# An encoder block's last two weight blocks of a chunk, multiplied two row tiles at a time

## The chip, the cores and the metric

The program runs on one core of one Trainium2 chip. The metric is the device time in microseconds (us) of one execution of the whole program. The engines are named as in the profile: PE (TensorE, matrix products), PEld (its weight loads), DVE (VectorE), ACT (ScalarE), POOL (GpSimd) and SP (SyncE, which here only issues DMAs). PE writes into PSUM, of which the kernel uses eight banks of 128 x 512 floats; all else lies in SBUF.

## The reference

One layer of a hybrid encoder on 512 tokens of width 2048, all in float32, cut to what matters:

```python
h = rmsnorm(x, g_mix)
qa, ka, va, qb, kb, vb = split(h @ w_in)             # w_in: 2048 x 4608
out_a = rmsnorm(mixer_a(qa, ka, va), g_out_a)        # 8 heads of 128, 2 kv heads, axial rotary
out_b = rmsnorm(mixer_b(qb, kb, vb), g_out_b)        # 8 heads, three dilated windows, partial rotary
x = x + concat(out_a, out_b) @ w_out                 # 2048 x 2048
gate, up = split(rmsnorm(x, g_ffn) @ w_gate_up)      # 2048 x 2 * 5632
x = x + (silu(gate) * up) @ w_down
return rmsnorm(x, g_final)
```

## The kernel before, in words

**Products.** Each float32 operand is split into a high and a low part of a faster type; ACT writes the high part (a copy that rounds), DVE the low part (the difference). A product is then three matmuls (`mm3`, L235 to L237). The 512 tokens are four row tiles of 128 (`NT = 4`). The work on PE is a list of *units*: one weight block of 128 rows by 512 columns against the four row tiles, twelve matmuls.

**Chunks.** A chunk is a run of units that add into the same four PSUM banks, one bank for each row tile. Units 0 to 63 are the four chunks qkB0 to qkB3 (`in_plain`, `in_chunk`), 16 units each: the queries and keys of two B heads per chunk. Units 64 to 95 are the four A chunks of W_out (`out_chunk` with kind "A"), 8 units each, A0 to A3. (The trace's chunks that are made of column blocks, before and behind these, are numbered apart.) Behind them come four B chunks of W_out, then the gate, up and down projections.

**Attention beside the chunks.** The attention of the 16 heads is cut into *head slots*, four a head. The loop at the end of the program runs a unit, then as many side tasks as a credit allows (1.42 a unit up to qkB3's end, 1.9 from A0 on, against a cost of 1.5 for a slot of an A head and 1.2 for one of a B head), so that one slot stands between most units, sometimes two, sometimes none. A slot issues, in this order: `pt` (four transposes of softmax rows, L582, into a bank; ACT copies it as `pTh`, L226, DVE makes `pTl`, L227), `pv` (three matmuls that add into the head's output bank), at a head's end `fin` (ACT: `oT` L599, its store L602, `sq` L608 or, for a mixer's first head, `acc` L605), `score` (three matmuls; for an A head DVE's maximum L567 and ACT's exponential L568, for a B head DVE's masked row L571 and ACT's exponential L573; then DVE's L575 and L576), and at times `tq` or `tk` (transposes of the next head's query and key, L544 and L555). The softmax rows of a slot are transposed six slots later, the transposed rows are multiplied two slots after that.

**What orders the work.** Each engine runs its instructions in the order of the program. `bank()` takes the oldest free bank from a queue of eight and `release` puts it at the end; a chunk holds four, a head's output one, and three are left for `pt`, `score`, `tq` and `tk`. A bank's next writer waits until its last reader is done. Small SBUF tiles (`slot`: p, pTh, pTl, qTh, oT, sq, acc, evqkB, x and so on) share one space; a tile takes the place of an older one, and its first writer waits until the older one's last reader is done, a DMA store among them.

**A chunk's end.** After the last unit all four banks are emptied in a row. A qkB chunk: ACT scales each bank in two halves into a tile evqkB (L467, L468), then issues its store to DRAM from its own queue (L457); from there the chunk is read back later as qkB. An A chunk: DVE multiplies each bank by the row's scale and adds x (L947, `scalar_tensor_tensor`). Each weight block is split beforehand: ACT L287, DVE L292.

Of the kernel before, what the change touches and what calls it, by code (L numbers as in the profile page):

```python
# [19 lines left out]
P = 128  # L20
# [3 lines left out]
NT = S // P  # L24
KD = D // P
# [43 lines left out]
def encoder_block(ctx, tc, x, g_mix, w_in, g_q_a, g_k_a, g_out_a, g_out_b, w_out, g_ffn,  # L69
# [163 lines left out]
    def mm3(dst, a, b, start, stop, chained=False):  # L233
        (ah, al), (bh, bl) = a, b
        nc.tensor.matmul(dst, ah, bh, start=start, stop=False, skip_group_check=chained)  # L235
        nc.tensor.matmul(dst, ah, bl, start=False, stop=False, skip_group_check=chained)  # L236
        nc.tensor.matmul(dst, al, bh, start=False, stop=stop, skip_group_check=chained)  # L237
# [4 lines left out]
    units = []  # L242
# [217 lines left out]
    def row_scale_of(name):  # L460
        return r1["rs" if name[:2] == "qB" else "r"]

    def post_plain(name, ps):
        for t in range(NT):
            e = homes.popleft() if name == "kvA" else slot("ev" + name)
            if name[:3] == "qkB":
                nc.scalar.activation(e[:, :256], ps[t][:, :256], AF.Copy, scale=r1["rs"][:, t:t + 1])  # L467
                nc.scalar.activation(e[:, 256:], ps[t][:, 256:], AF.Copy, scale=r1["r"][:, t:t + 1])  # L468
            else:
                nc.scalar.activation(e, ps[t], AF.Copy, scale=1.0 if name == "kvA" else r1["r"][:, t:t + 1])  # L470
            release(ps[t])
            store(name, t, e, nc.scalar)
            if name == "kvA":
                homes.append(e)
# [176 lines left out]
    def attention_tasks():  # L651
# [40 lines left out]
            todo += [weighed(cost, lambda s=s: head_slot(s))] + extra.get(s, [])  # L692
        return todo

    def add_chunk(w, rows, pieces, mm, post, early=None, side_in=None, dur=UNIT_US, tag="wd"):
        for j in range(0, len(rows), 2):
            m = 2

            def src_dst(t, j=j, m=m):
                t = t.rearrange("p (a c) -> p a c", c=512)  # L700
                return [(w_rows(w, rows[j], m, lo, n), t[:, :m, dst:dst + n]) for lo, dst, n in pieces]
            raw = Raw(src_dst)
            for s in range(m):
# [3 lines left out]
                units[-1].dur, units[-1].tag = dur, tag  # L707

    def in_chunk(pieces, post):
        box = {}  # L710

        def mm(u, k):
            if k == 0:
                box["ps"] = [bank() for _ in range(NT)]
            for t in range(NT):
                mm3(box["ps"][t], x_of(k, t), u.w, k == 0, k == KD - 1)
        add_chunk(w_in, [k * P for k in range(KD)], pieces, mm, lambda: post(box["ps"]), tag="wi")

    def first_chunk(lo, post):
        ps = []  # L720
# [153 lines left out]

    def in_plain(name, lo):
        pieces = [(QB + 256 * lo, 0, 256), (KB + 256 * lo, 256, 256)] if name[:3] == "qkB" else [(lo, 0, 512)]
        in_chunk(pieces, lambda ps: post_plain(name, ps))
# [29 lines left out]
    def out_chunk(kind, c):  # L907
        box = {}
        base = 0 if kind == "A" else NHA
        order = [6, 7, 0, 1, 2, 3, 4, 5] if (kind, c) == ("B", NC - 1) else list(range(NHA))  # L910

        def early(k):
            if (kind, k) not in oS:
                drain_until(lambda: (kind, k) in oT)
                oS[kind, k] = split(oT.pop((kind, k)), "oS", go[:, base + k:base + k + 1],
                                    at=O_HOMES["B"][2 * k:2 * k + 2] if k < 7 else None)

        class Back:
# [12 lines left out]
        def mm(u, n):  # L931
            k = order[n]
            if n == 0:
                box["ps"] = [bank() for _ in range(NT)]
                if kind == "A":
                    x1[c] = [slot("x1") for t in range(NT)]
                    for t in range(NT):
                        nc.sync.dma_start(x1[c][t], x[0, t * P:(t + 1) * P, c * 512:(c + 1) * 512])
            for t in range(NT):
                mm3(box["ps"][t], cols(oS[kind, k], t * P), u.w, n == 0, n == NHA - 1)  # L940

        def post():
            drain_until(lambda: kind in ro)
            if (kind, c) == ("B", 0):
                nc.scalar.activation(slot("table")[:, :1], ones, AF.Silu)
            for t in range(NT):
                nc.vector.scalar_tensor_tensor(x1[c][t], box["ps"][t], ro[kind][:, t:t + 1], x1[c][t],  # L947
                                               op0=OP.mult, op1=OP.add)
# [3 lines left out]
            if kind == "B":  # L952
                wait(1)
                if c == NC - 1:
                    side.extend(lambda p=p: h_side(2 * c, p, True) for p in range(4))
                    side.append(lambda: [square_x1(c, t) for t in (0, 1)])
                    side.extend(lambda p=p: h_side(2 * c + 1, p, True) for p in range(2))
                    side.append(lambda: park_x1(c))
                    side.append(lambda: [square_x1(c, t) for t in (2, 3)])
                    side.extend(lambda p=p: h_side(2 * c + 1, p, True) for p in range(2, 4))  # L960
                    side.append(make_r2)
                    return
                for i in (2 * c, 2 * c + 1):
                    for part in range(3):
                        side.append(lambda i=i, part=part: h_side(i, part))
                side.append(lambda: park_x1(c))
        add_chunk(w_out, [(base + k) * P for k in order], [(c * 512, 0, 512)], mm, post,
                  early if kind == "B" else None,
                  (lambda k: [Back(k)] if kind == "A" or k < SPILL_B else []) if c == 0 else None, tag="wa" if kind == "A" else "wo")

# [402 lines left out]
```

## Time and profile before

| | |
|---|---|
| median of three runs | 2019.24 us (2017.82 to 2020.35) |
| the profiled execution | 2017.83 us, of which the profile's span is 2016.0 us |
| PE busy | 1987.8 us, 99% of the span |
| DVE busy | 1573.0 us, 78% |
| ACT busy | 1113.6 us, 55% |
| qkB chunks, units 0 to 63 | end on PE at 264.8, 324.0, 396.3 and 472.8 us |
| A chunks, units 64 to 95 | end on PE at 524.6, 572.1, 605.1 and 626.9 us |

Times in the views are counted from the start of the span. A row of the timeline gives start, duration, engine, line, operation, output<-inputs with their buffer numbers left out, and in brackets how long the engine had been idle and whose end released it. All of PSUM's banks are called b. "evqkB" is an eviction of a qkB chunk, "qkB<-evqkB" its store. ACTq and SPq are DMA issues from the queues of ACT and SP. A small caution: a matmul of 512 columns is shown as 0.39 us busy, but starts 0.23 us after the one before it, so time lost to a wait is read from the distance of two starts, less 0.23.

### The profile page before, as it was taken

What the parts mean: (1) busy time and instruction counts of PE and PEld (TensorE: products, weight loads), DVE (VectorE), ACT (ScalarE), POOL (GpSimd) and SP (SyncE); (2) the same over time, 40 slices, a digit from 0 to 9 for tenths busy, and PEclk for the clock granted to TensorE, in tenths of its full rate; (3) what the DMA queues carried; (4) which work ended last, traced back from release to release, by engine and by line L of the source; (5) the groups of instructions that cost most, each with busy time, mean ns of one, the idle gap of its engine ahead of it and who ended that gap; (6) DMA issues with size and microseconds to landing.
All of it is one profiled execution on the core that took longest, in us unless ns stands there. A gap on an engine that the chain in (4) does not pass through costs nothing. (4 is left out here: it accounts for less than half of the span.)

```text
span 2016.0 us, 27418 instructions
## 1 busy us (share of the span) xinstructions
PE 1987.8 (99%) x9019; PEld 1632.0 (81%) x9019; DVE 1573.0 (78%) x2781; ACT 1113.6 (55%) x1972; POOL 153.2 (8%) x172
## 2 busy tenths in 40 slices
PE   9999999999999999999999999999999999999998
PEld 6788887887788888888888888888888888788886
DVE  7988866576754688878877878778788987977967
ACT  7655345455543565555555555545545666666656
POOL 4200100000010000000000000000000121111121
PEclk9999999999999999999999999999999999999999
DMA  8576533335244545747647558458367699779865
GB/s 268 188 261 221 186 115 103 109 116 168 89 151 141 188 163 199 242 134 266 219 165 274 182 182 289 148 202 297 120 241 241 202 252 271 185 176 271 201 156 164
DMA packets 231391, 390.61 MB, mean 194 GB/s; under 512 B 21408, under 2 KB 70352, under 8 KB 231120
## 3 DMA queue, kind: packets, MB, share of 16 engines
q1 hardware_dynamic: 204880, 326.13, 48.3%
q0 software_dynamic: 14960, 33.04, 8.0%
q10 hardware_dynamic: 11408, 29.70, 4.2%
q8 instruction: 70, 1.15, 0.2%
q14 instruction: 73, 0.60, 0.1%
HBM read 325.08 MB, written 63.70 MB: 193 GB/s over the span
## 5 line engine op out<-in xcount | busy, mean ns | idle before, releaser
L235 PE MATMUL b<-tw,arena 128*128 128x512 f32 x2136 | 838.1, 392 | 2.2 <-ACT ev L1139 2.2
L237 PE MATMUL b<-tw,arena 128*128 128x512 f32 x2136 | 833.5, 390 | 2.8 <-DVE arena L332 2.6
L236 PE MATMUL b<-tw,arena 128*128 128x512 f32 x2136 | 833.2, 390 | 2.2 <-DVE tw L764 1.9
L761 ACT ACTIVATE tw<-raw 128x512 fp32r<-128x512 f32 x924 | 559.1, 628 | 440.4 <-DVE raw L801 284.8
L764 DVE TENSOR_TENSOR tw<-raw,tw 128x512 fp32r<-128x512 f32 x924 | 619.2, 687 | 170.8 <-ACT tw L761 167.5
L237 PEld LDWEIGHTS b<-tw,arena 128*128 128x128 f32 x2136 | 401.2, 188 | 89.9 <-DVE arena L332 6.1
L236 PEld LDWEIGHTS b<-tw,arena 128*128 128x128 f32 x2136 | 401.6, 188 | 88.0 <-DVE tw L764 5.9
L235 PEld LDWEIGHTS b<-tw,arena 128*128 128x128 f32 x2136 | 401.5, 188 | 84.3 <-ACT ev L1139 2.9
L801 DVE TENSOR_TENSOR raw<-raw,raw 128x512 f32<-128x512 f32 x528 | 361.5, 685 | 2.8 <-DMA raw<-in_w_gate_up_dram 2.6
L1140 POOL DMA_DIRECT2D x1d<-ev x76 | 66.4, 975 | 1150.7 <-ACT ev L1139 1138.6
L235 PE MATMUL b<-w,arena 128*128 128x512 f32 x368 | 146.1, 397 | 0.0
L237 PE MATMUL b<-w,arena 128*128 128x512 f32 x368 | 143.8, 391 | 0.0
L236 PE MATMUL b<-w,arena 128*128 128x512 f32 x368 | 143.4, 390 | 0.0
L237 PEld LDWEIGHTS b<-w,arena 128*128 128x128 f32 x368 | 69.1, 188 | 15.0
L236 PEld LDWEIGHTS b<-w,arena 128*128 128x128 f32 x368 | 69.2, 188 | 13.8
L235 PEld LDWEIGHTS b<-w,arena 128*128 128x128 f32 x368 | 69.1, 188 | 13.6
L761 ACT ACTIVATE tw<-stage 128x512 fp32r<-128x512 f32 x90 | 54.5, 628 | 42.2 <-DVE stage L801 33.8
L227 DVE TENSOR_TENSOR pTl<-b,pTh 128x512 fp32r<-128x512 f32 x64 | 44.0, 687 | 34.3 <-ACT pTh L226 24.0
L292 DVE TENSOR_TENSOR w<-raw,w 128x512 fp32r<-128x512 f32 x96 | 64.8, 684 | 6.0 <-ACT w L287 3.2
L355 DVE TENSOR_TENSOR pair<-pair 128x256 f32<-128x256 f32 x120 | 45.5, 421 | 26.5 <-ACT pair L996 25.5
L226 ACT ACTIVATE pTh<-b 128x512 fp32r<-128x512 f32 x64 | 38.0, 594 | 46.6 <-PE b L582 41.7
L1139 ACT ACTIVATE ev<-b,smalls 128x512 f32<-128x512 f32 x76 | 49.5, 682 | 25.4 <-PE b L237 25.3
(197 smaller groups left out, 1820.7 us busy)
## 6 DMA issues: line engine op xcount, KB each, us to landing
raw<-in_w_gate_up_dram SPq DMA_DIRECT2D x616, 256.0 KB, 5.3
raw<-in_w_down_dram SPq DMA_DIRECT2D x176, 256.0 KB, 6.9
stage<-in_w_in_dram SPq DMA_DIRECT2D x106, 256.0 KB, 4.6
forms<-pair SPq DMA_DIRECT2D x22, 896.0 KB, 5.3
x1d<-ev POOLq DMA_DIRECT2D x76, 256.0 KB, 6.6
fr<-forms ACTq DMA_DIRECT2D x35, 512.0 KB, 5.9
raw<-in_w_in_dram SPq DMA_DIRECT2D x64, 256.0 KB, 5.5
raw<-in_w_out_dram SPq DMA_DIRECT2D x32, 512.0 KB, 4.6
```

The costliest lines, as they stand in the source:

```text
L226: nc.scalar.activation(hi, src, AF.Copy)
L227: nc.vector.tensor_tensor(lo, src, f32(hi), op=OP.subtract)
L235: nc.tensor.matmul(dst, ah, bh, start=start, stop=False, skip_group_check=chained)
L236: nc.tensor.matmul(dst, ah, bl, start=False, stop=False, skip_group_check=chained)
L237: nc.tensor.matmul(dst, al, bh, start=False, stop=stop, skip_group_check=chained)
L292: nc.vector.tensor_tensor(self.w[1], self.src, f32(self.w[0]), op=OP.subtract)
L355: nc.vector.tensor_tensor(out, x, y, op=op)
L761: nc.scalar.activation(self.pair[:, 0], self.src, AF.Copy)
L764: nc.vector.tensor_tensor(self.pair[:, 1], self.src, f32(self.pair[:, 0]), op=OP.subtract)
L801: nc.vector.tensor_tensor(t[dst], t[src[0]], t[src[1]], op=OP.add if form == "m6" else OP.subtract)
L1139: nc.scalar.activation(e, box.bank_of(form)[t], AF.Copy, scale=r2["r"][:, row:row + 1])
L1140: nc.gpsimd.dma_start(x1_dram[2 * cb + j, row], e, accum_op=OP.add)
```

## The change

In the last two units of each qkB chunk and of each A chunk the two loops are exchanged. Before, the second last unit multiplies its weight block with row tiles 0 to 3, and the last unit does the same with the next block. Now the second last unit multiplies *both* blocks with row tiles 0 and 1, and the last unit both blocks with row tiles 2 and 3. Row tiles 0 and 1 are evicted, stored and their banks released right after the second last unit, rows 2 and 3 after the last. Each row tile's sum is made in the same order as before. The B chunks of W_out go through the same function with `apart=False` and keep their order. No instruction is added or removed on PE, ACT or DVE; the lines below the new function move down by 15 (L947 becomes L962).

```diff
-    def post_plain(name, ps):
-        for t in range(NT):
+    def post_plain(name, ps, rows=range(NT)):
+        for t in rows:
...
+    def by_rows(u, k, count, product, done_rows, apart=True):
+        if not apart or k < count - 2:
+            for t in range(NT):
+                product(k, u.w, t)
+            if k == count - 1:
+                done_rows(range(NT))
+            return
+        both = [(count - 2, u.w if k == count - 2 else units[u.at - 1].w),
+                (count - 1, u.w if k == count - 1 else units[u.at + 1].w)]
+        rows = range(2) if k == count - 2 else range(2, NT)
+        for t in rows:
+            for i, w in both:
+                product(i, w, t)
+        done_rows(rows)
...
         def mm(u, k):
             if k == 0:
                 box["ps"] = [bank() for _ in range(NT)]
-            for t in range(NT):
-                mm3(box["ps"][t], x_of(k, t), u.w, k == 0, k == KD - 1)
-        add_chunk(w_in, [k * P for k in range(KD)], pieces, mm, lambda: post(box["ps"]), tag="wi")
+            by_rows(u, k, KD, lambda i, w, t: mm3(box["ps"][t], x_of(i, t), w, i == 0, i == KD - 1),
+                    lambda rows: post(box["ps"], rows))
+        add_chunk(w_in, [k * P for k in range(KD)], pieces, mm, None, tag="wi")
...
-            for t in range(NT):
-                mm3(box["ps"][t], cols(oS[kind, k], t * P), u.w, n == 0, n == NHA - 1)
-
-        def post():
+            by_rows(u, n, NHA, lambda i, w, t: mm3(box["ps"][t], cols(oS[kind, order[i]], t * P), w, i == 0,
+                                                   i == NHA - 1), post, kind == "A")
+
+        def post(rows):
             drain_until(lambda: kind in ro)
...
-            for t in range(NT):
+            for t in rows:
                 nc.vector.scalar_tensor_tensor(x1[c][t], box["ps"][t], ro[kind][:, t:t + 1], x1[c][t],
                                                op0=OP.mult, op1=OP.add)
                 release(box["ps"][t])
```

What this does to the order, at three places. First PE, in the second half of the second last unit of qkB3 (w_3936 with w_3937 is the high and low part of the second last weight block, w_3979 with w_3980 of the last; arena holds the row tiles). Before:

```order
L235 MATMUL b_74<-w_3936,arena_84 128x512
L236 MATMUL b_74<-w_3937,arena_84 128x512
L237 MATMUL b_74<-w_3936,arena_84 128x512
L235 MATMUL b_75<-w_3936,arena_84 128x512
L236 MATMUL b_75<-w_3937,arena_84 128x512
L237 MATMUL b_75<-w_3936,arena_84 128x512
```

and now:

```order
L235 MATMUL b_78<-w_3936,arena_84 128x512
L236 MATMUL b_78<-w_3937,arena_84 128x512
L237 MATMUL b_78<-w_3936,arena_84 128x512
L235 MATMUL b_78<-w_3979,arena_85 128x512
L236 MATMUL b_78<-w_3980,arena_85 128x512
L237 MATMUL b_78<-w_3979,arena_85 128x512
```

Row tiles 2 and 3 (banks 74 and 75) stood there with one weight block; now row tile 1 (bank 78) gets both.

Second ACT, at the end of qkB3, from the first eviction on. Before:

```order
L467 ACTIVATE evqkB_377_4126<-b_78,smalls 128x256
L468 ACTIVATE evqkB_377_4126<-b_78,smalls 128x256
L457 DMA qkB_104<-evqkB_377_4126 128x512
L467 ACTIVATE evqkB_378_4130<-b_71,smalls 128x256
L468 ACTIVATE evqkB_378_4130<-b_71,smalls 128x256
L457 DMA qkB_104<-evqkB_378_4130 128x512
L467 ACTIVATE evqkB_379_4134<-b_74,smalls 128x256
L468 ACTIVATE evqkB_379_4134<-b_74,smalls 128x256
L457 DMA qkB_104<-evqkB_379_4134 128x512
L467 ACTIVATE evqkB_380_4138<-b_75,smalls 128x256
L468 ACTIVATE evqkB_380_4138<-b_75,smalls 128x256
L457 DMA qkB_104<-evqkB_380_4138 128x512
```

and now (the first two rows are the store of row tile 1 and a `pt` copy; before, that copy and the three rows below it stood ahead of all evictions):

```order
L457 DMA qkB_104<-evqkB_373_4083 128x512
L226 ACTIVATE pTh_4091<-b_77 128x512
L573 ACTIVATE p_4101,smalls<-p_4101,smalls 128x512
L287 ACTIVATE arena_84<-raw_3850 128x512
L229 ACTIVATE arena_85<-oback_4061,fixed 128x512
L467 ACTIVATE evqkB_379_4134<-b_74,smalls 128x256
L468 ACTIVATE evqkB_379_4134<-b_74,smalls 128x256
L457 DMA qkB_104<-evqkB_379_4134 128x512
L467 ACTIVATE evqkB_380_4138<-b_71,smalls 128x256
L468 ACTIVATE evqkB_380_4138<-b_71,smalls 128x256
L457 DMA qkB_104<-evqkB_380_4138 128x512
L226 ACTIVATE pTh_4146<-b_76 128x512
```

Two evictions with their stores moved ahead of one head slot's work on ACT; two are left between that slot and the next slot's pTh_4146.

Third DVE, at the end of A0 (x_388 to x_391 are the row tiles' outputs). Before:

```order
L227 TENSOR_TENSOR pTl_4531<-b_73,pTh_4530 128x512
L571 ISA p_4546,smalls<-b_72,mask 128x512
L571 ISA smalls 128x1
L575 RECIPROCAL smalls<-smalls 128x1
L576 TENSOR_SCALAR p_4546<-p_4546,smalls 128x512
L292 TENSOR_TENSOR arena_84<-raw_4106,arena_84 128x512
L947 SCALAR_TENSOR_TENSOR x_388_4177<-b_78,smalls,x_388_4177 128x512
L947 SCALAR_TENSOR_TENSOR x_389_4178<-b_71,smalls,x_389_4178 128x512
L947 SCALAR_TENSOR_TENSOR x_390_4179<-b_74,smalls,x_390_4179 128x512
L947 SCALAR_TENSOR_TENSOR x_391_4180<-b_75,smalls,x_391_4180 128x512
```

and now:

```order
L962 SCALAR_TENSOR_TENSOR x_388_4177<-b_77,smalls,x_388_4177 128x512
L962 SCALAR_TENSOR_TENSOR x_389_4178<-b_73,smalls,x_389_4178 128x512
L227 TENSOR_TENSOR pTl_4533<-b_78,pTh_4532 128x512
L571 ISA p_4548,smalls<-b_75,mask 128x512
L571 ISA smalls 128x1
L575 RECIPROCAL smalls<-smalls 128x1
L576 TENSOR_SCALAR p_4548<-p_4548,smalls 128x512
L292 TENSOR_TENSOR arena_84<-raw_4114,arena_84 128x512
L962 SCALAR_TENSOR_TENSOR x_390_4179<-b_74,smalls,x_390_4179 128x512
L962 SCALAR_TENSOR_TENSOR x_391_4180<-b_71,smalls,x_391_4180 128x512
```

The same ten instructions, with two evictions moved ahead of one slot's softmax work.

Since the rows' tiles are now allocated at two moments, the tiles that follow take other places in SBUF, and wait for other older tiles. Those that matter, by the addresses in the built programs: at qkB1's end the place of the second evqkB tile goes on to the next p (the place of the third went on to the next pTl before). At qkB2's end a pTl, the third evqkB tile and another pTl now take, one after the other, the places of the first, the second and the third evqkB tile (before, the place of the third went on to a pTl and that of the fourth to a sq). At qkB3's end the place of the third goes on to the next p (that of the first to a pTl before), and the acc of the first B head now takes the place of a tile that was read long before, where it took that of a pTl still to be read.

More of the change, by code (lines that the diff above doesn't have):

```diff
@@ L706, in add_chunk @@
                                   early and (lambda i=i: early(i)), side_in and side_in(i)))
-                units[-1].dur, units[-1].tag = dur, tag
+                units[-1].dur, units[-1].tag, units[-1].at = dur, tag, len(units) - 1
     def in_chunk(pieces, post):
@@ L876, in in_plain @@
         pieces = [(QB + 256 * lo, 0, 256), (KB + 256 * lo, 256, 256)] if name[:3] == "qkB" else [(lo, 0, 512)]
-        in_chunk(pieces, lambda ps: post_plain(name, ps))
+        in_chunk(pieces, lambda ps, rows: post_plain(name, ps, rows))
     first_chunk(1024, lambda ps: post_plain("kvA", ps))
@@ L938, in mm @@
                         nc.sync.dma_start(x1[c][t], x[0, t * P:(t + 1) * P, c * 512:(c + 1) * 512])
-            for t in range(NT):
-                mm3(box["ps"][t], cols(oS[kind, k], t * P), u.w, n == 0, n == NHA - 1)
-        def post():
+            by_rows(u, n, NHA, lambda i, w, t: mm3(box["ps"][t], cols(oS[kind, order[i]], t * P), w, i == 0,
+                                                   i == NHA - 1), post, kind == "A")
+        def post(rows):
             drain_until(lambda: kind in ro)
-            if (kind, c) == ("B", 0):
+            if (kind, c) == ("B", 0) and 0 in rows:
                 nc.scalar.activation(slot("table")[:, :1], ones, AF.Silu)
-            for t in range(NT):
+            for t in rows:
                 nc.vector.scalar_tensor_tensor(x1[c][t], box["ps"][t], ro[kind][:, t:t + 1], x1[c][t],
@@ L951, in post @@
                     square_x1(c, t)
-            if kind == "B":
+            if kind == "B" and NT - 1 in rows:
                 wait(1)
@@ L966, in post @@
                 side.append(lambda: park_x1(c))
-        add_chunk(w_out, [(base + k) * P for k in order], [(c * 512, 0, 512)], mm, post,
+        add_chunk(w_out, [(base + k) * P for k in order], [(c * 512, 0, 512)], mm, None,
                   early if kind == "B" else None,
```

## The prediction

> **What bounds the kernel now.** I read the page first.
>
> ```profile
> PE 1987.8 (99%) x9019; PEld 1632.0 (81%) x9019; DVE 1573.0 (78%) x2781; ACT 1113.6 (55%) x1972; POOL 153.2 (8%) x172
> ```
>
> PE is busy 99% of 2016.0 us, so nothing but PE's 28 idle microseconds can be won. The order of those 28 is what matters, hence two views next: PE busy time by stretch, and what PE waited for between 190 and 740 us, which holds all the chunks that change.
>
> ```profile
> 200.00:300.00 100.00, 100.00 (x460) 82.81 (x459) 76.66 (x215) 40.68 (x83) 10.58 (x12) 1.00 0.47 154
> 300.00:380.00 80.00, 78.69 (x383) 64.81 (x382) 50.51 (x110) 39.04 (x82) 6.10 (x5) 1.00 0.33 105
> 380.00:440.00 60.00, 59.38 (x291) 48.62 (x291) 40.61 (x101) 31.68 (x68) 3.64 (x3) 1.00 0.30 98
> 440.00:500.00 60.00, 55.58 (x269) 44.24 (x268) 40.93 (x97) 33.16 (x69) 2.58 (x3) 0.97 0.49 165
> 500.00:560.00 60.00, 56.49 (x282) 44.92 (x281) 44.45 (x107) 33.97 (x72) 4.38 (x4) 1.00 0.33 103
> 560.00:740.00 180.00, 179.96 (x845) 148.45 (x844) 107.73 (x183) 90.72 (x165) 6.06 (x5) 1.00 0.48 161
> ...
> PE b L582 <- DVE pTl L227: 5.0, 4, 2.4
> PE b L235 <- DVE pTl L227: 2.8, 4, 1.3
> ```
>
> The second number of a stretch is its length, the third PE's busy time. So qkB0's end (264.8) and the ends of A1, A2 and A3 (572.1, 605.1, 626.9) cost PE nothing: 0 there before and 0 after. The idle time lies at the ends of qkB1, qkB2 and qkB3 and behind qkB3 up to 547; 7.8 of it is waits for pTl, a step that stands behind the evictions on ACT. Each of these places is followed separately.
>
> **qkB1's end.** The last unit ends at 323.96.
>
> ```profile
> 323.66 0.47 ACT L467 ACTIVATE evqkB<-b,smalls 128x256 f32<-128x256 f32 x1
> ...
> 327.01 0.33 ACTq L457 DMA_DIRECT2D qkB<-evqkB  x1
> ...
> 328.63 0.60 ACT L226 ACTIVATE pTh<-b 128x512 fp32r<-128x512 f32 x1 [0.40 <-ACT evqkB L468]
> 330.39 0.69 DVE L227 TENSOR_TENSOR pTl<-b,pTh 128x512 fp32r<-128x512 f32 x1 [5.72 <-DMA qkB<-evqkB]
> 331.14 0.50 PE L235 MATMUL b<-arena,qTh 128*128 128x512 f32 x1 [1.31 <-DVE pTl L227]
> ...
> DMA to landing us min/median/max: 2.0/2.0/3.8
> ```
>
> ACT is taken for 5.0 us by four evictions, pTh comes behind them, and pTl waits for the place of the third evqkB tile, whose store was issued at 327.01 and landed 3.4 later. PE waits 1.31; the next matmul starts 1.48 late. Each row tile costs 1.24 us on ACT (327.01 to 328.25 between two stores). After the change only two stand before pTh, and the pTl no longer takes that place. But the p before takes the place of row tile 1's evqkB. That eviction waits, as pTh did at 320.03, for an oA store, so its own store is issued at about 320.9. The stores of this kind landed in 2.0 (median) to 3.8 us: at 322.9 to 324.7. The exponential that writes the p could start at about 323.3 (pTh, pTl, L567 ahead of it, 0.6 to 0.7 each), so it is late by 0 to 1.4. With qTh and a weight's high part (0.6 each) behind it, two evictions (2.5) and pTh, the pTl ends at 329.1 to 330.4, and PE, which would be there at 329.83 without its wait, stands 0 to 0.5. Gain 1.0 to 1.48; I take 1.2, near the median landing.
>
> **qkB2's end.**
>
> ```profile
> 400.31 0.33 ACTq L457 DMA_DIRECT2D qkB<-evqkB  x1
> 400.68 0.60 ACT L226 ACTIVATE pTh<-b 128x512 fp32r<-128x512 f32 x1 [0.40 <-ACT evqkB L468]
> ...
> 401.31 0.69 DVE L227 TENSOR_TENSOR pTl<-b,pTh 128x512 fp32r<-128x512 f32 x1 [4.69 <-ACT pTh L226]
> 402.06 0.50 PE L235 MATMUL b<-pTh,arena 128*128 128x512 f32 x1 [0.62 <-DVE pTl L227]
> 402.32 0.60 ACT L608 ACTIVATE sq<-b 128x512 f32<-128x512 f32 x1 [0.56 <-DMA qkB<-evqkB]
> ```
>
> PE loses 0.83, and 0.13 behind it. Now three steps wait for stores, one behind the other: a pTl for row tile 0's (issued at about 391.2), row tile 2's eviction for row tile 1's, the next pTl for row tile 2's (issued at 397.2 to 398.6). With 2.0 us a store the last pTl ends at 400.1 and PE does not wait: gain 0.96. With 3.8 it ends at 403.1: PE waits 1.7, a loss of 0.7 against before. The two units stand back to back here, and the last block's low part is needed 2.7 us sooner, about 0.2 before DVE has it: −0.2. The store at 400.31 landed at 402.32, in 2.0, so I take a gain of 0.4, between 0.76 and −0.9 but nearer the first.
>
> **qkB3's end**, the largest term.
>
> ```profile
> 473.90 0.47 ACT L467 ACTIVATE evqkB<-b,smalls 128x256 f32<-128x256 f32 x1 [0.62 <-PE b L236]
> ...
> 478.64 0.50 PE L235 MATMUL b<-arena,arena 128*128 128x512 f32 x1 [0.28 <-ACT evqkB L468]
> 478.99 0.60 ACT L226 ACTIVATE pTh<-b 128x512 fp32r<-128x512 f32 x1 [0.40 <-ACT evqkB L468]
> 479.62 0.69 DVE L227 TENSOR_TENSOR pTl<-b,pTh 128x512 fp32r<-128x512 f32 x1 [3.65 <-ACT pTh L226]
> 480.37 0.65 PE L582 MATMUL b<-fixed,p 128*128 128x128 f32 x4 [0.76 <-DVE pTl L227]
> ...
> 486.20 0.60 ACT L605 ACTIVATE acc<-b 128x512 f32<-128x512 f32 x1 [1.85 <-PE b L236]
> 486.85 0.50 PE L235 MATMUL b<-kTh,qTh 128*128 128x512 f32 x1 [0.45 <-ACT acc L605]
> 487.53 0.16 DVE L575 RECIPROCAL smalls<-smalls 128x1 f32<-128x1 f32 x1 [1.56 <-ACT p L573]
> 489.94 0.68 DVE L227 TENSOR_TENSOR pTl<-b,pTh 128x512 fp32r<-128x512 f32 x1
> 490.67 0.66 PE L582 MATMUL b<-fixed,p 128*128 128x128 f32 x4 [2.42 <-DVE pTl L227]
> ```
>
> The first eviction waits for PE's last read of a pTl whose place it takes. Then four run, each freeing a bank that A0's first unit waits for, then pTh, then DVE after 3.65 idle. From there on the question is whether PE's time or DVE's carries the end. DVE by waits, and busy, from 479.6 to 546.0:
>
> ```profile
> 479.60:546.00 66.40, 60.03 (x289) 47.36 (x288) 48.89 (x116) 36.81 (x76) 3.86 (x3) 0.97 0.45 146
> ...
> DVE smalls L575 <- ACT p L573: 13.3, 14, 1.6
> ```
>
> Busy 48.9 and 13.3 for the exponential that DVE itself has set off (14 times, 0.88 at its shortest) make 62.2 of 66.4. DVE's order is a chain without slack there, while PE idles 6.4 us in the same stretch, but for the 0.45 at 486.85 always for DVE. So what this place gains is how far DVE's pTl at 479.62 moves, plus what disappears inside the chain. Now row tiles 2 and 3 remain: the eviction at 473.90 waits as before, two of 1.24 end at 476.4, pTh and pTl follow at 476.5 and 477.1: 2.5 earlier. The acc takes an old place, so its wait of 1.85 ends and DVE's 1.56 falls to the usual 0.88: 0.7. Against it, the p of the next slot waits for row tile 2's store: issued at 474.8, landing at 476.8 to 478.6, and wanted at 477.7: 0 to 0.9. Gain 2.3 to 3.2, and I take 3.1, by the 2.0 landing. The head slot that moves behind row tiles 0 and 1 on ACT has pTh at about 469.7 instead of 468.92; ACT had idled 2.5 before it, and DVE came to that pTl only at 470.00, so at most 0.3, which the 3.65 covers.
>
> PE also ran slowly after its longest wait:
>
> ```profile
> 490.70:494.70 4.00, 4.00 (x13) 3.24 (x14) 3.08 (x8) 2.30 (x5) 0.00 (x0) 0.59 0.30 114
> ```
>
> 13 matmuls in 4.0 us where the usual spacing of 0.23 gives 17, at a granted clock of 0.59: about 1.4 us. After the change this wait is 1.8 to 2.4, so the dip may stay or go. I count it 0 either way, since DVE's chain decides until 546. The Trainium skill, "TensorE: Matmul & The Clock Gate", Part 1 (the HAM clock gate), has the clock halved after at least one idle window of about 3.4 us. By that rule a wait of 2.42 would not do it, the dip would not hang on this wait, and the sum stays at −4.6; by the row the dip follows the wait, and if it went and counted, the sum would be −6.0.
>
> **A0's end.**
>
> ```profile
> 523.16 0.68 DVE L227 TENSOR_TENSOR pTl<-b,pTh 128x512 fp32r<-128x512 f32 x1
> ...
> 526.54 2.71 DVE L947 SCALAR_TENSOR_TENSOR x<-b,smalls,x 128x512 f32<-128x512 f32 x4
> ...
> 527.34 0.50 PE L235 MATMUL b<-arena,arena 128*128 128x512 f32 x1 [0.36 <-DVE x L947]
> ...
> 546.77 0.65 PE L582 MATMUL b<-fixed,p 128*128 128x128 f32 x4 [1.28 <-DVE pTl L227]
> ```
>
> DVE runs up to 4 us behind PE, so two evictions (1.4) ahead of a pTl make that pTl 1.4 later, and the two behind it come no sooner. DVE's sum is unchanged. PE may lose 0.2 at the pTl and wait to about 528.8 for row tile 2's bank instead of 527.34 for row tile 0's, but it waits for DVE again at 532.68, 534.49 and 546.77. Loss 0 to 0.7 (from DVE's 1.4, half of it lost if the exponential's round trip shifts); I take 0.1. At 546.77 a pTh waits for the oB store of the head before, a wait that stays.
>
> **Sum.** −1.2 −0.4 −3.1 +0.1 = −4.6. From 547 to the end PE has no room and no order changes, so it carries through. The profiled execution, 2017.83 (2016.0 and 1.83 outside), becomes 2013.2; the median run stands 1.41 above it, so 2014.6, −0.23%. The ends of the terms: −1.48 −0.76 −3.2 = −5.4, and −1.0 +0.9 −2.3 +0.7 = −1.7; that is 2013.8 to 2017.5. A difference of 0.2%, 4.04 us, is about what a measurement of this kernel can tell from none, so my value lies just past that bound, at 2015.2.
>
> **Rivals.**
> (1) The new slot waits eat most of it. Stores landing in 3.8 rather than 2.0 at all three places, as one in this stretch did: the near end of the sum, −1.7, 2017.5. For it: the wait at 330.39 was such a store. Against: median 2.0. Chance 0.36, for any outcome from 2015.2 to 2023.3; it would show as pTl or p released by a store.
> (2) Slower: qkB2's chain of stores. Its two pTl waits follow each other, so beyond 3.8 each microsecond of landing costs two. The longest landing beside these is the oB store of head 0:
>
> ```profile
> oB<-oT ACTq DMA_DIRECT2D x1, 256.0 KB, 8.0
> ```
>
> At 8.0 the place costs 0.9 + 2 × 4.2 = 9.3, less 1.2 and 3.1 elsewhere: +5.0, 2024.2. It turns slower by 0.2% from a landing of 7.5. Against it: only 0.29 of the DMA time is used around there. Chance 0.12, with others of its kind not seen.
> (3) More: the dip at 491 goes, and PE's own time turns out to be the path up to 515: −1.4 more, 2013.2; with the far ends 2012.4. Chance 0.1.
> (4) The evictions stay hidden and nothing changes, 2019.2: only if the waits above were not due to ACT; the four rows with "<-ACT evqkB" speak against it. It is within (1).
>
> **Chances.** My own forecast, 2013.8 to 2015.2, 0.42; with (3), faster 0.52; within 0.2%, 0.36; slower 0.12. The range 2011.5 to 2020.5 leaves out (2) and a little at the fast side, the end of (3) with the run-to-run 1.3 of before taken off and the same added above (1) and (4).
>
> **What would show it.** The changed profile should show no wait at PE for pTl at qkB1's end above 0.5; at qkB2's end none, or pTl released by a store; at qkB3's end pTh 2.5 us after the first late eviction, not 5.1, no wait of ACT for acc, and a wait of about 2 before the pt after it; at A0's end, four evictions in two pairs on DVE. I am wrong if DVE's chain starts no sooner, or if a store stands where ACT stood.

## The result

The changed kernel takes 2015.54 us (median; 2014.05 to 2018.23) against 2018.79 for the kernel before, measured beside it. The ratio is 0.9985, with a 95% interval of 0.9979 to 0.9991: about 3.0 us, or 0.15%, faster. The profiled execution took 2016.21 us, with a span of 2014.4. The sign is the forecast one and the time lies in the range. The sum of the terms was 4.6 us, the value given 4.0 (2015.2 against 2019.24), both at about the 0.2% bound or past it, and the gain stayed inside it. That 2015.54 lies 0.3 from 2015.2 is in part luck: the kernel before, too, measured 0.45 less than at the time of the forecast.

The waits of PE between 190 and 740 us, changed kernel (total, count, longest):

```profile
PE b L582 <- DVE pTl L227: 4.2, 3, 2.5
PE b L235 <- DVE pTl L227: 1.3, 3, 0.5
PE b L235 <- DVE x L962: 1.1, 1, 1.1
```

and PE's busy time by stretch, the answer to the table of the prediction (start and end, length, PE busy, and so on):

```profile
300.00:380.00 80.00, 80.00 (x392) 66.18 (x391) 51.74 (x108) 39.18 (x83) 6.10 (x5) 1.00 0.33 107
380.00:440.00 60.00, 59.44 (x290) 48.35 (x289) 40.18 (x101) 31.43 (x67) 3.88 (x3) 1.00 0.29 98
440.00:500.00 60.00, 57.39 (x284) 47.03 (x283) 43.44 (x103) 36.88 (x76) 2.53 (x3) 0.97 0.55 177
500.00:560.00 60.00, 55.84 (x278) 44.40 (x277) 43.90 (x107) 32.51 (x69) 5.01 (x4) 1.00 0.31 97
```

The wait at qkB1's end is gone (78.69 of 80 busy became 80.00), the one at qkB2's end is as large as it was, qkB3 gained, and the stretch of A0 lost: PE now waits 1.1 for an eviction on DVE, 0.36 before. The places one by one, from the timeline of the changed kernel (in its trace PE is 0.5 us earlier at 251 us already, which is no part of the change). First qkB1's and qkB2's ends:

```profile
320.51 0.33 ACTq L457 DMA_DIRECT2D qkB<-evqkB  x1
322.83 0.69 ACT L568 ACTIVATE p<-b,smalls 128x512 f32<-128x512 f32 x1 [1.35 <-DVE smalls L567]
327.25 0.60 ACT L226 ACTIVATE pTh<-b 128x512 fp32r<-128x512 f32 x1 [0.40 <-ACT evqkB L468]
...
389.63 0.33 ACTq L457 DMA_DIRECT2D qkB<-evqkB  x1
393.75 0.69 DVE L227 TENSOR_TENSOR pTl<-b,pTh 128x512 fp32r<-128x512 f32 x1 [3.37 <-DMA qkB<-evqkB]
399.45 0.69 DVE L227 TENSOR_TENSOR pTl<-b,pTh 128x512 fp32r<-128x512 f32 x1 [2.14 <-ACT pTh L226]
400.19 0.50 PE L235 MATMUL b<-pTh,arena 128*128 128x512 f32 x1 [0.53 <-DVE pTl L227]
```

At qkB1's end the p of 322.83 waited for DVE and not for the store of 320.51. At qkB2's end the pTl of 393.75 did wait for a store, that of row tile 0, issued at 389.63, 4.1 us before. Then qkB3's end and A0's:

```profile
474.66 0.60 ACT L226 ACTIVATE pTh<-b 128x512 fp32r<-128x512 f32 x1 [0.40 <-ACT evqkB L468]
475.29 0.69 DVE L227 TENSOR_TENSOR pTl<-b,pTh 128x512 fp32r<-128x512 f32 x1 [0.50 <-ACT pTh L226]
...
480.43 0.60 ACT L605 ACTIVATE acc<-b 128x512 f32<-128x512 f32 x1 [0.40 <-ACT oT L599]
...
482.53 0.17 DVE L575 RECIPROCAL smalls<-smalls 128x1 f32<-128x1 f32 x1 [0.88 <-ACT p L573]
...
485.68 1.12 PE L582 MATMUL b<-fixed,p 128*128 128x128 f32 x4 [2.49 <-DVE pTl L227]
...
518.04 1.40 DVE L962 SCALAR_TENSOR_TENSOR x<-b,smalls,x 128x512 f32<-128x512 f32 x2
519.36 0.68 DVE L227 TENSOR_TENSOR pTl<-b,pTh 128x512 fp32r<-128x512 f32 x1
520.33 0.40 PE L237 MATMUL b<-pTh,vl 128*128 128x512 f32 x1
520.53 0.60 ACT L608 ACTIVATE sq<-b 128x512 f32<-128x512 f32 x1 [2.35 <-PE b L236]
520.77 0.69 DVE L571 CUSTOM_DVE_ANT_0 p<-b,mask 128x512 f32<-128x512 f32 x1 [0.73 <-PE b L237]
524.35 0.50 PE L235 MATMUL b<-arena,arena 128*128 128x512 f32 x1 [1.10 <-DVE x L962]
528.38 0.66 PE L582 MATMUL b<-fixed,p 128*128 128x128 f32 x4 [0.55 <-DVE qTl L227]
```

At A0's end DVE itself stands idle: 0.73 before the step that writes p, a masked row. That wait had no counterpart before. It is not for the score that the row reads, which PE had done by 516.9. The L237 that releases it is the last matmul of the pv at 519.78, which reads pTh (520.33 and 0.40 more). By the addresses in the built program p takes the place of just that pTh in the changed kernel, as the sq at 520.53 takes that of the pTl beside it. In the kernel before, p takes the place of a pTl that PE had read by 514.6, 9 us sooner, and waits for nothing. So the reordering moved a place, and the new holder waits for PE to leave it.

And one thing happened where nothing was expected, a thousand microseconds behind the change, in the down projection:

```profile
1692.61 1.15 ACT L776 ACTIVATE tw<-raw 128x512 fp32r<-128x512 f32 x2 [7.90 <-DMA raw<-in_w_down_dram]
1693.30 0.50 PE L235 MATMUL b<-tw,arena 128*128 128x512 f32 x1 [1.68 <-ACT tw L776]
```

A W_down load came so late that PE waited 1.68 for the split of its weight. In the two first traces the change had given 4.2 us up to 1605 us, and 2.6 of them were lost between 1605 and 1732.

### The profile page after: what moved, and what is told of

The parts are those of the page before. It is cut to its first block, busy times and chain, and to the rows that moved or that the text cites. A ratio compares the mean times of both kernels' runs of the same rounds, so it can differ in the third digit from the quotient of the medians.

```text
span 2014.4 us, 27421 instructions
## 1 busy us (share of the span) xinstructions
PE 1984.7 (99%) x9019; PEld 1630.5 (81%) x9019; DVE 1573.3 (78%) x2781; ACT 1113.9 (55%) x1972; POOL 154.0 (8%) x172
## 5 line engine op out<-in xcount | busy, mean ns | idle before, releaser
L237 PE MATMUL b<-tw,arena 128*128 128x512 f32 x2136 | 833.0, 390 | 2.8 <-DVE arena L332 2.5
L237 PEld LDWEIGHTS b<-tw,arena 128*128 128x128 f32 x2136 | 401.0, 188 | 89.6 <-DVE arena L332 6.1
L237 PE MATMUL b<-w,arena 128*128 128x512 f32 x368 | 143.9, 391 | 0.0
L237 PEld LDWEIGHTS b<-w,arena 128*128 128x128 f32 x368 | 69.1, 188 | 15.0
L287 ACT ACTIVATE w<-raw 128x512 fp32r<-128x512 f32 x96 | 58.2, 622 | 14.0 <-PE b L236 8.1
```

The source lines that it names most:

```text
L287: nc.scalar.activation(self.w[0], src, AF.Copy)
```

## The experiments

Two distances, each between two matmuls that are the same instructions in every kernel, say more than the totals: **attention**, from the first matmul of 512 columns behind the eight transposes at 251 us (in qkB0) to PE's wait at 543 (in A1, the 1.28 at 546.77 of the kernel before), and **down**, from PE's wait for an eviction at 1605 to the like one at 1732, both "<-ACT ev". Between 543 and 1605 all fourteen traces agree within 0.6 us (1061.81 to 1062.40). Times in us; the totals are medians, the ratios are to the kernel before as measured beside each.

| kernel | attention | down | total | ratio (95%) |
|---|---|---|---|---|
| before | 294.86 | 127.23 | 2018.79 | 1 |
| changed | 291.04 | 129.84 | 2015.54 | 0.9985 (0.9979 to 0.9991) |
| e1_after_again | 291.45 | 127.30 | 2014.47 | 0.9983 (0.9974 to 0.9992) |
| e2_qkB_only | 290.57 | 124.93 | 2010.97 | 0.9966 (0.9954 to 0.9979) |
| e3_A_only | 295.59 | 125.59 | 2016.92 | 0.9995 (0.9986 to 1.0004) |
| e4_order_only | 293.37 | 127.32 | 2016.80 | 0.9998 (0.9989 to 1.0007) |
| e5_spare_tile | 295.05 | 126.89 | 2018.11 | 0.9997 (0.9988 to 1.0006) |
| e6_own_tiles | 290.50 | 127.30 | 2014.91 | 0.9982 (0.9973 to 0.9991) |
| e7_fill_wait | 290.00 | 125.72 | 2012.01 | 0.9968 (0.9956 to 0.9980) |
| e8_A0_not | 289.86 | 125.52 | 2011.35 | 0.9961 (0.9946 to 0.9976) |
| f1_before_spare | 294.88 | 124.67 | 2016.37 | 0.9987 (0.9978 to 0.9996) |
| f2_after_spare | 290.95 | 124.91 | 2012.34 | 0.9967 (0.9954 to 0.9979) |
| f3_qkB_two_spares | 290.36 | 127.09 | 2013.33 | 0.9977 (0.9968 to 0.9986) |
| f4_no_qkB2 | 290.16 | 124.89 | 2010.74 | 0.9961 (0.9947 to 0.9975) |

**The changed kernel once more.** No edit.

> The changed kernel once more, for a second trace of it. In the first pair of traces the chunks gave 4.0 us (PE at the same matmul of A3's end: 717.20 against 721.69, of which 0.52 stands already at 251 us), and 2.3 of it were lost again behind 1690 us, in the down projection, where PE waited 1.7 for a weight whose load came late. Theory 1 (that late load is chance, or a matter of one execution): this trace keeps about 4 us up to the end, no new wait of 1.5 at 1690 to 1700, total 4.0 below before. Theory 2 (the loads of W_down are bound by the DMAs there, so a PE that comes earlier waits for them): the same wait again, total 1.5 to 2.5 below before.

Up to 543 the trace is like the first (291.45), and the late load did not come again: 127.30 in the down stage, as in the kernel before. So the 1.68 was a matter of one execution. But the total is no more than 3.6 below before (2018.07 beside it).

**The two halves.** In e2 the last argument of `by_rows` in `out_chunk` is False, in e3 that in `in_chunk`; e8 leaves only A0 in the old order.

```diff
e2: -        ... post, kind == "A")
e2: +        ... post, False)
e8: +        ... post, kind == "A" and c > 0)
e3: -                    lambda rows: post(box["ps"], rows))
e3: +                    lambda rows: post(box["ps"], rows), False)
```

> Only the qkB chunks go by rows, the A chunks keep the old order. Theory: A0's part of the change costs 0.8 us, because two evictions ahead of a pTl make pv and score late and DVE's masked row waits 0.73 us for PE. Then PE's time from its wait at about 515 to its wait at about 528 (14.80 to 28.38 in the changed kernel, 13.58 us; 12.75 in the one before) is 12.75 again, DVE's L571 there waits for nothing, and the total is 4.8 us below before at A3's end. Rival: the 0.8 comes from where the qkB chunks leave DVE, and stays: 13.6.

> Only the A chunks go by rows. If A0's part alone costs: qkB1 to qkB3 as before (waits of 1.3, 0.6, 0.8 and 2.4 for pTl), and the stretch from the wait at about 520 to that at about 533 takes 13.6 us in place of 12.75; total 0.8 us above before, which timing will hardly tell from the same. If the 0.8 belongs to the combination alone: 12.75 and no difference.

> The changed kernel, but A0 in the old order. Theory (of the A chunks only A0 has a cost, since at A1 to A3 DVE and PE wait for nobody): up to 718 us the same as the qkB chunks alone, with 12.75 us between the waits at 516 and 529; whatever differs in the total comes from behind 1690 us. Rival (A1 to A3 cost or gain something): a difference of over 0.3 between 545 and 718.

In e3, where the A chunks alone go by rows, attention is 0.7 longer than before (295.59). A0's price is the same in all. From the wait at 516 (520 before) to that at 529 (533) it takes 12.75 us in the kernel before, 12.76 in e2 and e8 (516.34 to 529.10, 515.09 to 527.85); 13.58 and 13.54 in the changed kernel's two traces, and 13.57 in e3, where DVE's L571 waits 0.72 for PE. So A0 costs 0.8 us by its own, with or without the qkB chunks. The wait of L571 (0.69 to 0.73) is in the four traces with A0 by rows and in no other, and what is left of the 0.8 is 0.1. No run moves p's place alone, so that the place is the cause is read from the traces and the addresses; the text of e2 above still put it down to a late score. A1 to A3 cost nothing: from 543 to 718, behind the last B chunk, e2 takes 174.93 and e8 174.77. (The expectations call that point A3's end; A3 itself ends at about 627.) In attention the qkB chunks alone (e2, e8 and f3 below, mean 290.26) are 0.9 ahead of the changed kernel (291.04, 291.45 and 290.95). In e2 itself it was 4.3, not the 4.8 expected, with the slowest landing of qkB2's store among the traces. What no one had expected is the total: e2 is 3.5 below e1, and its down stage is 2.4 shorter than e1's.

**The order of the matmuls alone.**

```diff
                 product(i, w, t)
-        done_rows(rows)
+        if k == count - 1:
+            done_rows(range(NT))
```

> The matmuls go by rows as in the changed kernel, in qkB and A chunks, but all four evictions stay behind the last unit. If the gain comes from the evictions being in two pairs (theory), this is the kernel before, within 0.3 us at A3's end: ACT empties four banks in a row, the waits for pTl at the ends of qkB1, qkB2 and qkB3 are 1.3, 0.6 and 0.8. If it comes from the order of the matmuls or the earlier need of the last block, some of the 4.0 us shows here.

Neither: the waits for pTl are there (1.16, 0.62, 0.76), but attention is 1.5 shorter than before, all of it at qkB3's end.

```profile
473.42 0.46 ACT L467 ACTIVATE evqkB<-b,smalls 128x256 f32<-128x256 f32 x1
478.37 0.60 ACT L226 ACTIVATE pTh<-b 128x512 fp32r<-128x512 f32 x1 [0.40 <-ACT evqkB L468]
484.13 0.60 ACT L605 ACTIVATE acc<-b 128x512 f32<-128x512 f32 x1 [0.40 <-ACT oT L599]
```

The first eviction starts at once, where it waited 0.62 for PE to leave a tile, and acc waits for nothing, where it waited 1.85. So the tiles' other places in SBUF can by themselves give 1.5, about half of what qkB3 gained: 0.7 at acc and the rest up to the pTl, which comes at 479.00. In the changed kernel the first of these did not add to the gain. There the first late eviction starts 8.55 us behind the same matmul of PE as before (463.50 to 472.05, and 465.35 to 473.90), held up not by a place but by ACT, which comes to it that late behind the moved pair. The pTl is 2.48 earlier by the same measure (11.79 against 14.27), which is two evictions of 1.24, and acc's place gives the other 0.7.

**qkB2.** e6 is e2 with four tiles for the evictions of the qkB chunks alone; f4 is e2 with qkB2 in the old order.

```diff
e6: -            e = homes.popleft() if name == "kvA" else slot("ev" + name)
e6: +            e = homes.popleft() if name == "kvA" else (sp.tile([P, 512], F32, tag="eq", bufs=4, name=nm("ev" + name))
e6: +                                                       if name[:3] == "qkB" else slot("ev" + name))
f4: -        in_chunk(pieces, lambda ps, rows: post_plain(name, ps, rows))
f4: +        in_chunk(pieces, lambda ps, rows: post_plain(name, ps, rows), name != "qkB2")
```

> qkB chunks by rows, A chunks in the old order, and the evictions of the qkB chunks in four tiles of their own, so that no pTl, p or eviction stands right behind one of their stores. Theory (the gain that was forecast at qkB2's end was eaten by pTl's wait for the store of row tile 0, 3.4 us, which pushed everything behind it): the wait for pTl at about 401 us, 0.5 to 0.8 in the changed kernel, becomes 0 to 0.2, and PE is 0.6 to 0.9 us earlier from there to 463; total 0.5 to 0.9 below the qkB chunks alone, if the W_down stage is alike. Rival (ACT's queue is the limit there, two evictions and a softmax row): 0.5 to 0.8 again.

> qkB0, qkB1 and qkB3 by rows, qkB2 and the A chunks in the old order; the place goes to the later load. Theory (qkB2's part of the change is worth nothing): a wait of 0.6 at about 401 us as before, and up to 463 within 0.3 us of the qkB chunks alone; total within 0.5 of 2011. Rival (it still gives the 0.4 that was forecast): PE 0.4 later from 401 on.

In e6 the pTl no longer waits for a store, comes 1.3 to 1.4 earlier than in the changed kernel, and PE's wait for it is gone; another took its place:

```profile
392.45 0.69 DVE L227 TENSOR_TENSOR pTl<-b,pTh 128x512 fp32r<-128x512 f32 x1 [1.69 <-ACT pTh L226]
398.07 0.69 DVE L227 TENSOR_TENSOR pTl<-b,pTh 128x512 fp32r<-128x512 f32 x1 [2.21 <-ACT pTh L226]
400.56 0.60 ACT L609 ACTIVATE sq<-b 128x512 f32<-128x512 f32 x1 [2.03 <-PE b L236]
401.21 0.50 PE L235 MATMUL b<-arena,qTh 128*128 128x512 f32 x1 [0.45 <-ACT sq L609]
```

The sq now takes the place of a tile that PE still reads. So it is shown that the store held up the pTl, and the gain is not had: attention 290.50, no better than 290.26. And f4, without qkB2's part, stands at 290.16: that part is worth nothing, 0.1 the wrong way (0.2 between the same instructions, see below).

**PE's slow clock behind its longest wait.**

```diff
         def tq(self):
             ps = bank()
+            if (self.kind, self.h) == ("B", 4):
+                for _ in range(8):
+                    nc.tensor.matmul(ps, heads[11].q[0][:, :P], heads[11].k[0], start=True, stop=True)
```

> qkB chunks by rows, and eight matmuls whose result nobody reads put ahead of the transposes of the fifth B head's query, where PE waits 2.5 us for pTl: PE idles about 0.7 there instead of 2.5. Theory (DVE's chain sets the end up to 543 us, so PE's slow clock behind the wait costs nothing): the granted clock behind the wait is 1.0, PE's 1.3 to 1.5 us come back as longer waits for pTl at about 511 and 516, and PE's wait at about 543 ends at the same time; total the same. Rival (the slow clock is on the path): everything from there on 1.3 us earlier.

PE's wait fell from 2.49 to 0.66, and the four microseconds behind it ran at full clock (e2's answer to the same question had 0.57 and 13 matmuls):

```profile
485.60:489.60 4.00, 4.00 (x20) 3.38 (x21) 3.08 (x8) 2.31 (x5) 0.00 (x0) 1.00 0.31 95
```

Further on in its timeline:

```profile
499.13 0.50 PE L235 MATMUL b<-pTh,vh 128*128 128x512 f32 x1 [1.54 <-DVE pTl L227]
```

What PE had won it stood again at 499.13, for DVE; the waits had been expected at about 511 and 516. From the wait for qkB3's pTl (0.66, ended at 485.52) to the one in A1 at 541.48 it takes 55.96 us; in e2, with the slow clock, 56.03 (487.11 to 543.14). The slow clock costs 0.1 here. There are more witnesses, which no edit made: in e4, e5, e8 and f1 the same wait of 2.42 to 2.49 was followed by a full clock and by the 1.54 at about 500, and the distances are 55.92 to 56.00 there.

Where PE is the path it is another matter. In one trace, e6, the slow clock also came behind PE's wait at 1732, 1.67 long there as in the others. The four microseconds behind it, first in e6, then in e1:

```profile
1731.57:1735.57 4.00, 4.00 (x11) 3.13 (x12) 3.81 (x6) 3.03 (x5) 1.73 (x2) 0.57 0.97 253
1732.60:1736.60 4.00, 4.00 (x18) 3.30 (x19) 3.80 (x6) 3.03 (x5) 1.73 (x2) 1.00 0.93 259
```

The twentieth matmul behind the wait comes at 6.31 us in e6, at 4.65 to 4.69 in the other thirteen traces; the thousandth at 228.44, and at 226.79 to 226.82. There the slow clock costs 1.6, and none of it comes back.

**The down stage.** The edit of e5 is one unused tile at A0's start; f1 (on the kernel before) and f2 (on the changed one) have it at the first B chunk's, and f3 (on e2) two of them at A0's.

```diff
+                if (kind, c) == ("A", 0):                # e5, f3; ("B", 0) in f1 and f2
+                    nc.gpsimd.memset(slot("spare")[:, :1], 0.0)      # f3: twice
                 if kind == "A":
```

> The kernel before, in its old order, with one more small SBUF tile allocated at the start of A0 and one column of it set by POOL: the tiles behind it, the W_down weights among them, take other places. The waits at 1690 to 1720 have so far been 1.8 us in sum in the kernel before, 4.2 and 1.9 in the changed one (two executions), 1.9 with the order of the matmuls alone, 0.4 with the A chunks by rows, 0 with the qkB chunks by rows. Theory (they hang on which older tile a W_down load has to wait for, and on when DMAs land, not on the chunks): the waits at the ends of the chunks stay as before (1.3, 0.6, 0.8, 2.4 us), those at 1690 to 1720 come out otherwise than 1.8, anywhere from 0 to 4. Rival (they follow from the time at which PE comes there): 1.8 again.

e5 told nothing apart: its waits behind 1690 make PE's starts 1.5 later in sum, and its down stage takes 126.89, near the kernel before. The unused tile by itself changes nothing there. What separates the kernels then came from SP's longest wait for a weight tile's place in 1600 to 1720, and from the addresses. In before, changed, e1, e4, e5 and e6 SP stands 19.4 to 20.3 us for one place, with no load issued meanwhile; in e2, e3, e7 and e8 9.3 at most. In the first group, by the addresses in the built programs, the place of one W_down tile, which is split late, goes to a load six loads sooner than in the second, and holds up those behind it: in the kernel before, that load and four more went out within 2.42 us from 1661.59, the four with no wait of their own.

> The kernel before, in its old order, with one unused SBUF tile at the start of the first B chunk (one column set by POOL). By the addresses in the built program, the place of one W_down tile (the 7521st matmul group's last reader) is then taken six loads later than in the kernel before. In all nine traces so far these two cases fall into two groups: with the early load SP stands 19.4 to 20.3 us for that place and the stretch from PE's wait at about 1605 to that at about 1732 takes 126.9 to 129.8 us; with the later one SP's longest such wait is 9.3 and the stretch takes 124.9 to 125.7. Theory (the place alone decides): chunks as before, SP's longest wait 9.3, the stretch 125.0 to 125.8, total 1.5 to 2.5 us below before. Rival (the chunks' times decide): 19 to 20, 127, and no difference in total.

> The changed kernel with the same unused tile at the same point, which here too moves that place to the load six later. Theory: the chunks give their 3.8 to 4.2 us as in the two traces of the changed kernel, the stretch 1605 to 1732 takes 125.0 to 125.8, and the total is 5.5 to 6.5 us below the kernel before, and 3.6 to 4.6 below the kernel before with the unused tile, which is the price of the change by itself. Rival: no more than the 3.3 of the changed kernel.

> Qk chunks alone by rows, with two unused tiles at the start of A0, which move the place back to the early load. Theory: chunks 4.5 to 5.0 us ahead of before, SP's longest wait 19 to 20, the stretch 126.9 to 127.5, total 2.0 us above the qkB chunks alone: 2012.8 to 2014.0. Rival: 125, and 2011 in total.

All three came out on the side of the theory, two down stages and f3's longest wait just outside the figures expected (125.0 to 125.8, and 19 to 20). SP's waits in 1600 to 1720 for DVE to leave a place (total, count, longest), first the kernel before:

```profile
SPq L264 <- DVE tw L764: 33.3, 10, 19.8
```

then f1,

```profile
SPq L264 <- DVE tw L764: 21.5, 17, 9.3
```

and f3, which was moved the other way:

```profile
SPq L264 <- DVE tw L779: 30.5, 6, 18.6
```

The down stage takes 124.67, 124.91 and 127.09. Over all fourteen traces the early place gives 126.89 to 129.84, the late one 124.67 to 125.72, with no overlap, and f1 to f3 set it by an unused tile alone, with attention as it was. In totals: f1 is 1.9 below the kernel before (2018.22 beside it), f3 2.4 above e2. The changed kernel and the kernel before both have the early place, so this took no part in the measured 3.0. It is a part of why e2 and e8 looked so good.

The price of the change by itself, both kernels with the late place: 2012.34 against 2016.37, 4.0 us, from two ratios of 0.9967 and 0.9987 to the same kernel. Their intervals leave some 3 us to either side.

**The fastest.** f4, 2010.74, ratio 0.9961 (0.9947 to 0.9975), beats both kernels; e8 and e2 are its equals. Its 7.5 us are some 4.7 from qkB1 and qkB3 by rows, some 2 from the place in the down stage, and the rest is within the totals' spread.

## Why the prediction was right, and where not

By its own terms, each measured between the same instructions:

| term | forecast | measured |
|---|---|---|
| qkB1's end | −1.2 | −1.6 (328.53 to 334.68 is 6.15; 328.01 to 332.58 is 4.57) |
| qkB2's end | −0.4 | +0.25 (384.42 to 403.78 is 19.36; 382.32 to 401.93 is 19.61) |
| qkB3's end | −3.1 | −3.15 (465.35 to 504.29 is 38.94; 463.50 to 499.29 is 35.79) |
| A0's end | +0.1 | +0.83 (12.75 to 13.58) |
| attention in all | −4.6 | −3.8 (294.86 to 291.04) |

- **qkB1** was right in mechanism and 0.4 better than its sum: the store landed in 2.0, so the p did not wait for it, and the pTl of 327.88 found its place free.
- **qkB3** was right to 0.1, for the reasons given: two evictions fewer before pTh moved DVE's pTl 2.48 sooner, DVE's chain set the end from there, and acc's old place took DVE's wait of 1.56 to 0.88. Only "the eviction at 473.90 waits as before" did not hold: it starts as late, but because ACT comes to it that late.
- **qkB2 is the first step that failed**: "with 2.0 us a store the last pTl ends at 400.1", and "I take a gain of 0.4, between 0.76 and −0.9 but nearer the first". The evictions gave 0.1 where 0.6 was taken, and the low part of the last block that is needed sooner cost 0.3 where 0.2 was taken (384.42 to 400.83 is 16.41 in the kernel before, and 16.73 to 16.75 in all nine traces whose matmuls go by rows there). The store of row tile 0 held pTl up until 3.8 to 4.4 us after its issue in the seven traces that have it with shared tiles (4.1 in the first), where 3.8 was the far end. In these seven PE's wait for the later pTl is that time less 3.6, one for one: 3.82 and 0.21 in e8, 4.12 and 0.53 in the changed kernel, 4.37 and 0.77 in e2. So below about 3.6 there would be no wait, an estimate from these rows. Of the three waits that the text set one behind the other only this first one came: row tile 2's eviction and the next pTl found the stores landed.
- Why that store took 4 us where others take 2 can be read from SP's loads. SP issues the two loads of a weight block just ahead of it, here 1.6 and 1.2 us. DMA share, the last number but one of a row, in the 2 us behind the issue of that store, and behind the one of 397.20, which landed in 2.0:

```profile
388.00 0.88 SPq L264 DMA_DIRECT2D raw<-in_w_in_dram  x2
389.63:391.63 2.00, 2.00 (x13) 1.65 (x12) 0.75 (x2) 1.09 (x3) 0.00 (x0) 1.00 0.96 339
397.20:399.20 2.00, 2.00 (x11) 1.60 (x11) 0.11 (x1) 1.22 (x3) 0.00 (x0) 1.00 0.35 131
```

- All eight traces with that store (the seven, and e6) have a share of 0.95 to 0.97 there and 3.7 to 4.3 us to its landing. The kernel before showed both beforehand: its store of 325.77, 1.0 and 0.6 us behind two loads, landed in 3.8 at a share of 0.92, and where the text has row tile 0's store issued, at 391.2, two loads go out at 390.08 and behind, with a share of 0.86 in the 2 us from there. So the median landing and the mean share of 0.29 were the wrong rows. No run moves these loads, so this is read from the traces and not tested.
- **A0 is the second**: "loss 0 to 0.7 ... I take 0.1". The term for the order alone was right: 0.83 less DVE's wait of 0.73 is the 0.1. What it had put at nothing is that the moved steps get other places. It followed the places at the three qkB chunks, not here, where p took the place of a pTh that PE had just read. The round trip that the text named as the far end is not what happened: PE runs from 514.80 to 522.86 without a wait, and the score was there in time.
- **The slow clock** counted 0 "since DVE's chain decides until 546". e7 and the four traces without it show 0.1 or less there. Rival (3), which put it on the path, is out at this place: its 1.4 came back as a wait of 1.54. Its price is real where PE is the path, as at 1732 in e6.
- "From 547 to the end PE has no room and no order changes, so it carries through": 543 to 1605 carried through, within 0.4. Behind it the sentence was too sure, though the loss of the first trace (2.6) did not come again in e1 (0.1). The order is the same, but some tiles' places differ from build to build, and f1 to f3 show that these alone move the end by 2 us. That both kernels fell on the same side was luck that the text did not know it needed.
- Rival (1), stores that eat the gain, is true of qkB2 alone. Rivals (2) and (4) did not come.

So 4.6 became 3.8 in attention by two terms, qkB2 (0.65 off) and A0 (0.73 off), with 0.4 better at qkB1 and 0.2 between the places. The measured 3.0 has an interval of 1.8 to 4.2 us (0.0009 and 0.0021 of 2018.79), which holds 3.8. What is left between the two isn't told apart.

## What to carry to other kernels

First find the chain that sets the time in the stretch at hand: what moves its first step is gained in full, and what is off it, like half a clock on PE behind 490 us, costs next to nothing, though the same on it costs all of its 1.6. Where tiles share space, an edit also moves places. For each step that the edit moves, look up which tile's place it will take and who reads that tile last; with equal work in another order, that cost 0.7 here as the traces read.

A step that waits for a store is priced by the nearest like store, not by the median: see which loads go out just ahead of its issue, and read the DMA share of the two microseconds behind it, not the mean of the stretch.

A difference of a few microseconds between two builds may come from places far behind the edit. So compare distances between the same instructions, and put an unused tile in to see how much the places alone can do.

## What the runs showed of the hardware

PE's clock fell to 0.57 to 0.66 for some 4 us behind the wait of 2.42 to 2.49 us in nine of the thirteen traces that have it, and stayed at 1.00 in the other four, with the same wait. Behind the wait of 1.67 at 1732 it fell once in fourteen traces. The Trainium skill, "TensorE: Matmul & The Clock Gate", Part 1, has a free-running activity window of about 3.4 us. That the same wait halves the clock in one execution and not in the next agrees with a window that runs freely, but a wait well under its length was enough.

A store of the qkB chunks that was issued within 1.6 us behind two weight loads, with a DMA share of 0.92 to 0.97 in the 2 us that follow, landed in 3.7 to 4.3 us; the one at 397.20, with a share of 0.35, in 2.0.

And W_down loads stand for up to 20 us behind one place. SP issues its loads in order, and the load that waits for its place holds back those behind it: four of them went out right behind it at 1661.59, with no wait of their own.
